# The last step of an output product by accumulator, and the residual scaled half by half inside the product

## The chip, the cores and the metric

The kernel runs on one core of a Trainium2 chip. The metric is the device time of one execution in microseconds (us); the median of three runs stands for it. One execution was also recorded by the hardware profiler; all rows below are of it.

## The reference, cut to what matters

A diffusion transformer of two layers works on 512 tokens (x) and 256 context tokens, each 1024 wide. Every layer has a feed-forward network (FFN), a set of four mixers, and a second FFN. What concerns the change is how a sublayer's result is joined to the stream, and the FFN itself:

```python
ALPHA = (2 * DEPTH) ** 0.25

def post_norm(x, f, g, b):
    return layer_norm(ALPHA * x + f, g, b)

def swiglu(h, w_in, w_out):
    a, u = jnp.split(h @ w_in, 2, axis=-1)
    return (jax.nn.silu(a) * u) @ w_out
```

So after each sublayer the stream x is scaled by ALPHA, the sublayer's output f (multiplied by a row of the modulation) is added, and the sum is normalised with a gain g and a bias b. D_FF is 2816, which is 22 chunks of 128.

## The kernel before, in words

The stream lies in SBUF as six tiles of 128 tokens by 1024, `res`: t0 to t3 hold x, t4 and t5 the context. The last FFN works on x alone, with four tiles.

All products are in fp32 by three matmuls each: every operand is split into a high part and the rest, and `mm3` (L335 to L337) issues high times high, high times low, low times high. For weights the split is made on the fly: SP loads `wraw` (two buffers), ScalarE (ACT) casts `wh` (L328), VectorE (DVE) subtracts to give `wl` (L329); there are six slots of each. GpSimd (POOL) adds and subtracts weight tiles in the FFN's input product, which uses a fast scheme with sums of tiles (`first`, `winograd`, L573, L608 to L616); its results are combined on DVE (L692 to L703).

`ffn` runs the 22 chunks in parts: 0 to 4, 4 to 8, 8 to 12, 12 to 16, 16 to 18 and 18 to 22 (the last FFN: 0 to 6, 6 to 12, 12 to 18, 18 to 22). For each chunk it makes the gated product and stores it as `gTh` (ACT, L646) and `gTl` (DVE, L647). After each part but the last it calls `branch_out`, the output product of this part: for each half of 512 columns (dh 0, then 1), steps of two chunks; in each step for both chunks, for all tiles, three matmuls. Six accumulators are open in a half: t0 and t1 in single-bank PSUM tiles (`psp`, two buffers), t2 and t4 in one two-bank tile and t3 and t5 in another (`ps`, two buffers). When a half's matmuls are issued, `add` follows for each tile: DVE multiplies the accumulator by the modulation row (L472) and adds the result to `res` (L474). There are 15 such calls in the four FFNs. The merges behind the mixers call the same function.

The residual of a sublayer is the normalised stream, scaled. Normalisation without gain and bias goes to the next product; `res` is brought to ALPHA times (x g + b) by `rescale`: two gain rows are loaded (L451), scaled on ACT (L460), and then for both halves and all tiles DVE multiplies and adds (L465), 24 instructions with six tiles, 16 with four. For the kernel's first sublayer `scale_input` only multiplies by ALPHA (L359, six instructions of 1024 columns). Either one is a generator kept as `self.behind`, and `ffn` runs it to its end ahead of its first output product:

```python
            if lo == 0:
                for _ in self.behind(pool, tiles):
                    pass
```

The order of each engine is not written by hand: a scheduler walks the program and puts an instruction where its operands and buffers are thought to be ready, so what stands late in the code can run early. That is how the scaling got to the start of the FFN, between the casts of the next stream (L391, L392), the small rows of the normalisation (L398 to L436) and the combinations of the input product. Each engine then runs its own order strictly, and waits at an instruction whose operands or buffers are not ready.

In the third mixer (`gqa`) small tables of cosines times gain are made on POOL (L862, L866), twelve instructions in all.

## Time and profile before

| | us |
|---|---|
| median of three runs | 2946.29 |
| lowest and highest | 2943.25, 2949.76 |
| the profiled execution | 2945.09 |
| its span in the profile | 2943.3 |
| PE busy | 2844.5 (97%) |
| DVE busy | 2062.5 (70%) |
| ACT busy | 1196.5 (41%) |
| POOL busy | 460.5 (16%) |
| mean granted clock of TensorE | 0.991 of full speed |

PE (TensorE) is busy nearly always, so the table says little; the places where it waits, and for whom, are read from the list of waits and the timelines in the section on the rows. Two hints for them: a matmul of 512 columns is shown with 0.39 us or so, but matmuls overlap and start 0.23 us apart; and an idle time in brackets names the engine, tile and line that ended it.

### The profile page before, as it was taken

What the parts mean: (1) busy time and instruction counts of PE and PEld (TensorE: products, weight loads), DVE (VectorE), ACT (ScalarE), POOL (GpSimd) and SP (SyncE); (2) the same over time, 40 slices, a digit from 0 to 9 for tenths busy, and PEclk for the clock granted to TensorE, in tenths of its full rate; (3) what the DMA queues carried; (4) which work ended last, traced back from release to release, by engine and by line L of the source; (5) the groups of instructions that cost most, each with busy time, mean ns of one, the idle gap of its engine ahead of it and who ended that gap; (6) DMA issues with size and microseconds to landing.
All of it is one profiled execution on the core that took longest, in us unless ns stands there. A gap on an engine that the chain in (4) does not pass through costs nothing.

```text
span 2943.3 us, 43403 instructions
## 1 busy us (share of the span) xinstructions
PE 2844.5 (97%) x16220; PEld 2437.0 (83%) x16220; DVE 2062.5 (70%) x4278; ACT 1196.5 (41%) x2269; POOL 460.5 (16%) x342
## 2 busy tenths in 40 slices
PE   7999999999999999999999999999999999899997
PEld 4898888988787788888888789998988787788886
DVE  4766658775757787666676976776886767876558
ACT  4333233364456552322323523332344456443333
POOL 1222122100000012221121222221200000012112
PEclk9999999999999999999999999999999999999998
DMA  6453334231133313543444122222132242242332
GB/s 233 144 165 108 108 107 130 85 110 51 47 77 72 108 58 108 186 136 116 158 135 138 58 72 72 79 61 76 48 98 72 57 110 78 79 129 88 94 99 71
DMA packets 319207, 296.07 MB, mean 101 GB/s; under 512 B 16312, under 2 KB 244752, under 8 KB 318740
## 3 DMA queue, kind: packets, MB, share of 16 engines
q1 hardware_dynamic: 317939, 290.80, 31.9%
q0 software_dynamic: 1056, 2.49, 0.4%
q8 instruction: 128, 2.10, 0.3%
q14 instruction: 84, 0.68, 0.1%
HBM read 270.52 MB, written 7.39 MB: 94 GB/s over the span
## 4 chain that ended last, share of the span: by engine, by line
PE 78%; DVE 14%; issue 3%; ACT 2%; DMA 2%; POOL 0%; SPq 0%; DVEq 0%; ACTq 0%; POOLq 0%
PE ps L335 12%; PE ps L337 12%; PE ps L336 12%; PE psp L335 9%; PE psp L337 9%; PE psp L336 9%; PE ps L260 2%; PE ps L1033 2%; PE ps L1075 2%; PE psp L1091 2%; DVE wl L329 2%; DVE tmp L472 2%; DVE res L465 2%; DVE res L474 1%; DVE actl L392 1%
## 5 line engine op out<-in xcount | busy, mean ns | idle before, releaser
L328 ACT CAST wh<-wraw 128x512 fp32r<-128x512 f32 x570 | 352.3, 621 | 874.0 <-PE ps L337 454.9
L329 DVE TENSOR_TENSOR wl<-wraw,wh 128x512 fp32r<-128x512 f32 x570 | 414.8, 733 | 323.7 <-ACT wh L328 316.3
L335 PE MATMUL psp<-acth,wh 128*128 128x384 f32 (+2 forms) x1432 | 482.1, 337 | 8.3 <-DVE e L701 3.8
L336 PE MATMUL psp<-actl,wh 128*128 128x384 f32 (+2 forms) x1432 | 480.3, 336 | 4.8 <-DVE actl L392 4.7
L337 PE MATMUL psp<-acth,wl 128*128 128x384 f32 (+2 forms) x1432 | 478.6, 335 | 5.2 <-DVE wl L329 5.2
L335 PEld LDWEIGHTS psp<-acth,wh 128*128 128x128 f32 x1432 | 271.3, 190 | 48.9 <-issue 25.4
L328 ACT CAST wh<-wrax 128x512 fp32r<-128x512 f32 x280 | 173.8, 622 | 338.1 <-PE ps L336 198.0
L336 PEld LDWEIGHTS psp<-actl,wh 128*128 128x128 f32 x1432 | 271.7, 190 | 19.9 <-DVE actl L392 6.5
L337 PEld LDWEIGHTS psp<-acth,wl 128*128 128x128 f32 x1432 | 271.8, 190 | 17.7 <-DVE wl L329 5.8
L335 PE MATMUL ps<-S,wh 128*128 128x384 f32 (+1 forms) x840 | 275.9, 329 | 8.1 <-DVE e L692 5.3
L337 PE MATMUL ps<-S,wl 128*128 128x384 f32 (+1 forms) x840 | 275.1, 327 | 0.0
L336 PE MATMUL ps<-S,wh 128*128 128x384 f32 (+1 forms) x840 | 275.0, 327 | 0.0
L329 DVE TENSOR_TENSOR wl<-wrax,wh 128x512 fp32r<-128x512 f32 x280 | 214.1, 770 | 84.5 <-ACT wh L328 59.3
L335 PE MATMUL ps<-acth,wh 128*128 128x512 f32 (+2 forms) x688 | 245.8, 359 | 3.2 <-ACT wh L328 1.7
L336 PE MATMUL ps<-actl,wh 128*128 128x512 f32 (+2 forms) x688 | 244.3, 355 | 0.0
L337 PE MATMUL ps<-acth,wl 128*128 128x512 f32 (+2 forms) x688 | 243.5, 354 | 0.0
L335 PE MATMUL ps<-wh,gTh 128*128 128x512 f32 x594 | 234.9, 395 | 7.5 <-DVE tmp L472 7.5
L337 PE MATMUL ps<-wh,gTl 128*128 128x512 f32 x594 | 233.5, 393 | 0.0
L336 PE MATMUL ps<-wl,gTh 128*128 128x512 f32 x594 | 233.3, 393 | 0.0
L474 DVE TENSOR_TENSOR res<-res,tmp 128x512 f32<-128x512 f32 x268 | 188.0, 732 | 0.6
L335 PEld LDWEIGHTS ps<-S,wh 128*128 128x128 f32 x840 | 158.7, 189 | 12.9 <-issue 6.9
L336 PEld LDWEIGHTS ps<-S,wh 128*128 128x128 f32 x840 | 158.7, 189 | 0.0
(385 smaller groups left out, 5452.2 us busy)
## 6 DMA issues: line engine op xcount, KB each, us to landing
araw<-in_ada_w_dram SPq DMA_DIRECT2D x128, 512.0 KB
wraw<-in_ffn_w_out_dram SPq DMA_DIRECT2D x88, 512.0 KB
wrax<-in_ffn_w_in_dram SPq DMA_DIRECT2D x160, 256.0 KB
wraw<-in_ffn_w_in_dram SPq DMA_DIRECT2D x120, 256.0 KB
wraw<-in_mix_w_in_dram SPq DMA_DIRECT2D x44, 512.0 KB
wraw<-in_ffn_w_in_dram SPq DMA_DIRECT2D x36, 512.0 KB
wraw<-in_mix_w_out_dram SPq DMA_DIRECT2D x16, 512.0 KB
mrow<-mrow SPq DMA_DIRECT2D x10, 512.0 KB
```

The lines of the kernel that those rows point to most:

```text
L260: nc.tensor.matmul(ps[32 * g:32 * g + 32, :], lhsT=self.cs[:, k, c0:c0 + 32], rhs=w[:, k - kk, :], start=i == 0 and k < 4, stop=i == len(n ...
L328: self.nc.scalar.copy(h, raw)
L329: self.nc.vector.tensor_tensor(lo, raw, h.bitcast(F32), op=ALU.subtract)
L335: mm(out, lhsT=a[0], rhs=b[0], start=start, stop=False)
L336: mm(out, lhsT=a[0], rhs=b[1], start=False, stop=False)
L337: return mm(out, lhsT=a[1], rhs=b[0], start=False, stop=stop)
L465: nc.vector.tensor_tensor(r, r, x[:, lo:hi], op=op)
L472: nc.vector.tensor_tensor(y, acc, mrow[0 if t < 4 else 1][:, dh * 512:(dh + 1) * 512], op=ALU.mult)
L474: nc.vector.tensor_tensor(r, r, y, op=ALU.add)
L1033: nc.tensor.matmul(ps[:, at:at + hi - lo], lhsT=q, rhs=part[:, lo:hi], start=i == 0, stop=i == 1)
L1075: nc.tensor.transpose(pt[:, j * P:(j + 1) * P], p[:, a:a + P], self.ident)
L1091: nc.tensor.matmul(out[64 * a:64 * a + 64, :], lhsT=v[:, kt, vcol:vcol + 64], rhs=pT[:, i], start=i == 0, stop=i == len(order) - 1)
```

## The change

It has three parts. First, in the last step of a half in `branch_out` the matmuls are sorted by tile and then by chunk: each accumulator gets both chunks of the step one after the other. Second, `rescale` and `scale_input` are cut into a first piece (gain loads and ACT's scaling) and one piece for each half; `ffn` runs the first piece ahead of the first output product, and `branch_out` runs a half's piece behind the matmuls of that half and ahead of its additions, and not before the subtraction of the part's last `gTl` has been issued. `scale_input` now has twelve instructions of 512 columns. Third, the tables of the third mixer are made on DVE.

```diff
-    def scale_input(self, pool, tiles):
-        for r in self.res:
-            self.nc.vector.tensor_scalar(r, r, ALPHA, None, op0=ALU.mult)
+    def scale_input(self, pool, tiles, tags=None):
+        yield
+        for lo, hi in ((0, 512), (512, D)):
+            for t in tiles:
+                r = self.res[t][:, lo:hi]
+                self.nc.vector.tensor_scalar(r, r, ALPHA, None, op0=ALU.mult)
             yield
...
         for x in gb:
             nc.scalar.mul(x, x, ALPHA)
+        yield
         for lo, hi in ((0, 512), (512, D)):
...
-    def branch_out(self, l, i, tiles, steps, a_of, w_of, mrow, tmp, todo=None):
+    def branch_out(self, l, i, tiles, steps, a_of, w_of, mrow, tmp, todo=None, behind=None):
...
-                for j, k in enumerate(s):
-                    for t in tiles:
-                        self.mm3(acc[t], a_of(k, t), w[j], k == chunks[0], k == chunks[-1])
+                by_step = [(t, j) for j in range(len(s)) for t in tiles]
+
+                for t, j in sorted(by_step) if s is steps[-1] else by_step:
+                    self.mm3(acc[t], a_of(s[j], t), w[j], s[j] == chunks[0], s[j] == chunks[-1])
+            if behind:
+                with self.tc.issue_after(behind[1].ins):
+                    next(behind[0])
...
-                store(g, f, lo)
+                end = store(g, f, lo)
+            behind = None
             if lo == 0:
-                for _ in self.behind(pool, tiles):
-                    pass
+                behind = self.behind(pool, tiles, ("mrow0", "mrow1") if self.side else ("mrow1", "mrow2")), end
+                next(behind[0])
...
-            nc.gpsimd.tensor_tensor(tc_, cos, bcast1(gain, 4), op=ALU.mult)
+            nc.vector.tensor_tensor(tc_, cos, bcast1(gain, 4), op=ALU.mult)
...
-                nc.gpsimd.tensor_tensor(t5[:, :, :, f], s5[:, :, :, f], bcast1(g5[:, :, 1 - f], 8), op=ALU.mult)
+                nc.vector.tensor_tensor(t5[:, :, :, f], s5[:, :, :, f], bcast1(g5[:, :, 1 - f], 8), op=ALU.mult)
```

Three places show how the orders move. In the changed kernel the same code has other line numbers: L465 becomes L469, L472 L476, L474 L478, L392 L395, L402 L405. The first place is on PE, the beginning of the last step of the first half in the first output product of the kernel. The names end in running numbers; two `wh` numbers are the two chunks of the step, `psp` and `ps` the accumulators. Before:

```order
474 L335 MATMUL psp_1029<-wh_1081,gTh_395 128x512
475 L336 MATMUL psp_1029<-wl_1082,gTh_395 128x512
476 L337 MATMUL psp_1029<-wh_1081,gTl_396 128x512
477 L335 MATMUL psp_1030<-wh_1081,gTh_395 128x512
478 L336 MATMUL psp_1030<-wl_1082,gTh_395 128x512
479 L337 MATMUL psp_1030<-wh_1081,gTl_396 128x512
480 L335 MATMUL ps_197_1031<-wh_1081,gTh_395 128x512
481 L336 MATMUL ps_197_1031<-wl_1082,gTh_395 128x512
482 L337 MATMUL ps_197_1031<-wh_1081,gTl_396 128x512
```

Each accumulator gets three matmuls of the first chunk and then the next one's turn comes. The same place on PE after the change:

```order
474 L335 MATMUL psp_1023<-wh_1075,gTh_395 128x512
475 L336 MATMUL psp_1023<-wl_1076,gTh_395 128x512
476 L337 MATMUL psp_1023<-wh_1075,gTl_396 128x512
477 L335 MATMUL psp_1023<-wh_1079,gTh_395 128x512
478 L336 MATMUL psp_1023<-wl_1080,gTh_395 128x512
479 L337 MATMUL psp_1023<-wh_1079,gTl_396 128x512
480 L335 MATMUL psp_1024<-wh_1075,gTh_395 128x512
481 L336 MATMUL psp_1024<-wl_1076,gTh_395 128x512
482 L337 MATMUL psp_1024<-wh_1075,gTl_396 128x512
```

The matmuls of the second chunk (1079) moved up behind those of the first, so the first accumulator has all its matmuls after six. The second place is on DVE, near the start of the second FFN, before; `rs` are the small rows of the normalisation, `mrow` the scaled gain and bias:

```order
1613 L465 TENSOR_TENSOR res_2001_9931<-res_2001_9931,mrow_2220_11217 128x512
1614 L403 SCALAR_TENSOR_TENSOR rs_2110_10540<-rs_2110_10540,rs_2108_10538 128x2
1615 L465 TENSOR_TENSOR res_2002_9932<-res_2002_9932,mrow_2220_11217 128x512
1616 L404 SCALAR_TENSOR_TENSOR rs_2109_10539<-rs_2110_10540,rs_2109_10539 128x2
1617 L465 TENSOR_TENSOR res_2001_9931<-res_2001_9931,mrow_2221_11218 128x512
1618 L402 TENSOR_TENSOR rs_2110_10540<-rs_2109_10539 128x2
```

Scaling stands between the rows of the normalisation. The same place on DVE after the change:

```order
1622 L329 TENSOR_TENSOR wl_10692<-wraw_10685,wh_10691 128x512
1623 L405 TENSOR_TENSOR rs_2110_10546<-rs_2109_10545 128x2
1624 L406 SCALAR_TENSOR_TENSOR rs_2110_10546<-rs_2110_10546,rs_2108_10544 128x2
1625 L407 SCALAR_TENSOR_TENSOR rs_2109_10545<-rs_2110_10546,rs_2109_10545 128x2
1626 L405 TENSOR_TENSOR rs_2110_10546<-rs_2109_10545 128x2
```

All 24 scaling instructions of this FFN moved from its start. The third place is where they went: DVE in the first output product of the second FFN. Before, from the part's last `gTl` to the additions of the first half:

```order
1732 L647 TENSOR_TENSOR gTl_10606<-ffg_11072,gTh_10605 128x768
1733 L329 TENSOR_TENSOR wl_11418<-wraw_11415,wh_11417 128x512
1734 L329 TENSOR_TENSOR wl_11422<-wraw_11415,wh_11421 128x512
1735 L329 TENSOR_TENSOR wl_11493<-wraw_11486,wh_11492 128x512
1736 L472 TENSOR_TENSOR tmp_11347<-psp_11251,mrow_2222_11247 128x512
1737 L472 TENSOR_TENSOR tmp_11350<-psp_11252,mrow_2222_11247 128x512
1738 L474 TENSOR_TENSOR res_2001_9931<-res_2001_9931,tmp_11347 128x512
1739 L474 TENSOR_TENSOR res_2002_9932<-res_2002_9932,tmp_11350 128x512
1740 L472 TENSOR_TENSOR tmp_11353<-ps_2226_11253,mrow_2222_11247 128x512
```

After the change, where the last `gTl` is row 1719 and the half's twelve scaling instructions are rows 1720 to 1731:

```order
1730 L469 TENSOR_TENSOR res_2005_9941<-res_2005_9941,mrow_2221_11224 128x512
1731 L469 TENSOR_TENSOR res_2006_9942<-res_2006_9942,mrow_2221_11224 128x512
1732 L476 TENSOR_TENSOR tmp_11341<-psp_11233,mrow_2222_11229 128x512
1733 L476 TENSOR_TENSOR tmp_11344<-psp_11234,mrow_2222_11229 128x512
1734 L478 TENSOR_TENSOR res_2001_9937<-res_2001_9937,tmp_11341 128x512
1735 L478 TENSOR_TENSOR res_2002_9938<-res_2002_9938,tmp_11344 128x512
1736 L329 TENSOR_TENSOR wl_11412<-wraw_11409,wh_11411 128x512
1737 L329 TENSOR_TENSOR wl_11416<-wraw_11409,wh_11415 128x512
1738 L469 TENSOR_TENSOR res_2001_9937<-res_2001_9937,mrow_2220_11223 128x512
1739 L476 TENSOR_TENSOR tmp_11347<-ps_2226_11235,mrow_2222_11229 128x512
```

The scaling moved in between `gTl` and the first multiply, and the two weight subtractions of the second half (`wl_11412` and `wl_11416`, before `wl_11418` and `wl_11422`) moved behind the first two additions.

## Rows read from the trace of the kernel before

**Rows 1.** The page: busy time, share, instructions; and the chain that ended last.

```profile
PE 2844.5 (97%) x16220; PEld 2437.0 (83%) x16220; DVE 2062.5 (70%) x4278; ACT 1196.5 (41%) x2269; POOL 460.5 (16%) x342
...
PE 78%; DVE 14%; issue 3%; ACT 2%; DMA 2%; POOL 0%; SPq 0%; DVEq 0%; ACTq 0%; POOLq 0%
```

**Rows 2.** PE's waits by releaser: us in total, times, longest.

```profile
PE ps L335 <- DVE tmp L472: 8.6, 16, 0.8
PE ps L335 <- DVE e L692: 5.3, 4, 1.9
PE psp L335 <- DVE e L701: 5.2, 5, 1.9
PE psp L337 <- DVE wl L329: 5.2, 2, 3.0
PE psp L336 <- DVE actl L392: 4.7, 6, 1.6
...
PE ps L335 <- DVE ffg L642: 2.8, 1, 2.8
```

**Rows 3.** Timeline of DVE, first product of FFN 1: start, us, instruction, count.

```profile
128.65 1.28 DVE L472 TENSOR_TENSOR tmp<-psp,mrow 128x512 f32<-128x512 f32 x2
...
133.35 1.28 DVE L474 TENSOR_TENSOR res<-res,tmp 128x512 f32<-128x512 f32 x2
134.55 1.27 DVE L472 TENSOR_TENSOR tmp<-ps,mrow 128x512 f32<-128x512 f32 x2
```

**Rows 4.** Timeline of PE at the second half, FFN 1 and FFN 2.

```profile
134.17 0.39 PE L336 MATMUL psp<-wl,gTh 128*128 128x512 f32 x1
135.28 0.50 PE L335 MATMUL ps<-wh,gTh 128*128 128x512 f32 x1 [0.72 <-DVE tmp L472]
135.62 0.39 PE L336 MATMUL ps<-wl,gTh 128*128 128x512 f32 x1
...
1158.15 0.39 PE L335 MATMUL psp<-wh,gTh 128*128 128x512 f32 x1
...
1162.10 0.50 PE L335 MATMUL ps<-wh,gTh 128*128 128x512 f32 x1 [0.53 <-DVE tmp L472]
```

**Rows 5.** Timeline of DVE at the start of FFN 2: two groups of scaling.

```profile
1078.76 3.08 DVE L465 TENSOR_TENSOR res<-res,mrow 128x512 f32<-128x512 f32 x5
...
1116.88 0.68 DVE L465 TENSOR_TENSOR res<-res,mrow 128x512 f32<-128x512 f32 x1
```

**Rows 6.** Timeline of PE at the start of FFN 2: two of its waits.

```profile
1088.37 0.39 PE L336 MATMUL psp<-actl,wh 128*128 128x256 f32 x1 [1.11 <-DVE actl L392]
...
1106.82 0.44 PE L337 MATMUL psp<-acth,wl 128*128 128x384 f32 x1 [2.18 <-DVE wl L329]
```

**Rows 7.** By stretch: us, busy PE, PEld, DVE, ACT, POOL, granted clock, DMA, GB/s.

```profile
1082.00:1104.00 22.00, 19.84 (x134) 17.71 (x134) 22.00 (x42) 15.23 (x34) 7.27 (x5) 1.00 0.09 25
1104.00:1118.00 14.00, 10.10 (x48) 9.46 (x46) 12.17 (x18) 6.04 (x11) 7.94 (x5) 0.88 0.39 114
...
1682.00:1694.00 12.00, 9.47 (x44) 9.15 (x44) 10.18 (x13) 5.46 (x10) 7.26 (x5) 0.86 0.34 101
...
2600.00:2631.00 31.00, 28.42 (x181) 26.23 (x182) 22.66 (x40) 12.78 (x24) 7.42 (x5) 0.94 0.49 155
```

**Rows 8.** Timeline of PE in the one-step product of FFN 3.

```profile
2066.62 0.79 PE L337 MATMUL psp<-wh,gTl 128*128 128x512 f32 x1 [1.22 <-DVE gTl L647]
2067.21 0.63 PE L335 MATMUL psp<-wh,gTh 128*128 128x512 f32 x1
```

**Rows 9.** Timeline of DVE in the first product of FFN 2.

```profile
1144.48 0.96 DVE L647 TENSOR_TENSOR gTl<-ffg,gTh 128x768 fp32r<-128x768 f32 x1 [0.30 <-ACT gTh L646]
...
1156.66 2.38 DVE L474 TENSOR_TENSOR res<-res,tmp 128x512 f32<-128x512 f32 x2
```

**Rows 10.** Timeline of POOL in the first product of FFN 2.

```profile
1155.21 1.49 POOL L608 TENSOR_TENSOR wraw<-wraw,wraw 128x512 f32<-128x512 f32 x1 [18.49 <-DMA wraw<-in_ffn_w_in_dram]
```

**Rows 11.** POOL's groups: one of the four of tables; busy, mean ns.

```profile
L866 POOL TENSOR_TENSOR tab<-cst,kn 128x256 f32<-128x256 f32 x4 | 4.2, 1066 | 0.9 <-DVE tA L802 0.9
```

More of the change, by code (lines that the diff above doesn't have):

```diff
@@ L646, in store @@
             nc.scalar.copy(gh, g)
-            nc.vector.tensor_tensor(gl, g, gh.bitcast(F32), op=ALU.subtract)
+            return nc.vector.tensor_tensor(gl, g, gh.bitcast(F32), op=ALU.subtract)
         def first(late):
@@ L736, in ffn @@
                                                .rearrange("(j p) c -> p j c", p=P), (2, 512)),
-                    mrow, pool)
+                    mrow, pool, behind=behind)
                 continue
```

## Prediction

> **What bounds the kernel now.** I read the page first. TensorE (PE) is busy for 97% of the span and PE alone makes up 78% of the chain that ended last; VectorE (DVE) makes up 14% of it [rows 1]. So this is a kernel that runs matmuls nearly all the time, and any gain must come out of the short stretches in which PE waits. I went next to the list of PE's waits and took from it the six that the change can touch [rows 2]; all six end on DVE. They fall into two kinds.
>
> The first kind is the 8.6 us in 16 waits for the multiply of L472 (accumulator times modulation row). They stand where an output product goes from its first half of 512 columns to its second. In the first product of the first feed-forward network (FFN) DVE's rows read as a queue: t0 and t1 multiplied, added, then t2 and t3, and only from 134.55 the multiplies of t4 and t5 [rows 3]. Tiles t2 and t4 share one two-bank PSUM tile, so the second half's t2 cannot start before t4's multiply is done: PE starts a matmul at 134.17 and the next at 135.28 [rows 4]. Between two starts there are 0.23 us on an undisturbed stretch, so this wait costs 1.11 - 0.23 = 0.88 us, and 0.11 more in the matmul after it (0.34 between starts), 0.99 in all against the 0.72 that the row shows as idle. I add 0.28 us per wait for this wherever I use idle times. In the second FFN the same place is 0.53 idle [rows 4].
>
> The second kind is DVE's backlog at the start of an FFN. There the scaling of the residual stands between work that PE needs: in the second FFN five scaling instructions in a row end at 1081.8 in front of the casts, and others alternate with the sums of the FFN's input product [rows 5]. The table by stretch has DVE busy for all 22.00 us from 1082 to 1104 [rows 7], and PE waits for it at 1088.37 and 1106.82, 1.11 and 2.18 us, among others [rows 6].
>
> **Part 1, the last step by accumulator.** It adds and removes no instruction; 36 matmuls of the last step stand in another order. Before, t0 is complete after 21 of them and t5 after 36, three matmuls (0.69 us) apart; now t0 is complete after 6 and each next one 1.4 us later. DVE takes about 1.2 us for one accumulator (a pair of multiplies takes 1.28, a pair of additions the same when nothing disturbs it [rows 3]), so it keeps pace and the queue is gone: t4 is complete 1.4 us before the end of the half, its multiply ends some 0.5 us before or up to 0.6 after that end, depending on the additions in between, and PE wants that tile after seven more matmuls, 1.6 us after the end. t5's has 2 us. The waits of this kind should vanish. 16 x 0.28 + 8.6 = 13.1 us are there; one of the 16 (0.8 us) belongs to the second merge, whose DVE queue holds a scaling that stays, which leaves 12.3. In the first product of each of the four FFNs the scaling now stands in the queue, and I count half of their waits (four of about 0.8, so 1.6 us) as kept: **10.7 us gained**. Bounds 7 (nothing in first products, and a fifth of the rest kept) and 12.3.
>
> **Part 2, the scaling leaves the starts.** The scaling itself hardly changes: 24 instructions per FFN with six tiles, 16 with four, 0.60 us from start to start (five took 3.08 [rows 5]); in the first FFN six of 1024 columns become twelve of 512. What counts is the place. From the starts of the second and third FFN 14.4 us of DVE work goes, from the fourth 9.6. The waits that end on this backlog are four for e of L692 (5.3 us), five for e of L701 (5.2; two of them, 1.9 each, at FFN starts, so I take 3.8), two for wl (5.2), six for actl (4.7) and one for ffg (2.8) [rows 2]: 21.8 us in 15 waits, with 0.28 each 26.0. To that comes TensorE's clock. In the stretch from 1104 to 1118, after idling 2.18 us, PE was granted 0.88 of full speed on average; the stretches at 1682 and 2600 show 0.86 and 0.94 [rows 7]. A mean of 0.88 of 2.4 GHz is 24% of 14 us at the 1.2 GHz level, which loses half of 3.4 us, 1.7; the other two lose 1.7 and 1.9. Together 31.3 us. Not all of it will be had, because a removed wait uncovers the next one: ACT's casts (a weight's wl waits for wh on its row all through the kernel), POOL's sums of weights, and the FFN's own latency from product to gate to product. DVE loses 38.4 us of work in the three stretches to save 31, and it was busy without a gap there, so most should come through; I take 85%: **27 us gained**, bounds 13 (the next wait ends half as late) and 31.
>
> **What part 2 costs where it goes.** In the first product of the second FFN the last gTl ends at 1145.4 [rows 9], 4 us after the product's first matmul (1141.5; the second half starts at 1158.2, which is 72 matmuls of 0.23 later). Then DVE runs the 12 instructions of the half, 7.2 us, until 1152.6. t0 and t1 are complete at 1151.2 and 1152.6, so the multiplies start without delay; two multiplies and two additions bring DVE to 1155.0, and the two weight subtractions that now stand behind them to 1156.2, ahead of 1158.2, when PE's second half reads the first of them. t2, t3 and t4 follow with two scaling instructions of the second half mixed in, and t4's multiply ends at about 1159.9; PE wants its tile at 1159.8. So the cover is used up but hardly overdrawn. I charge 0.5 us per FFN, **2 us** in all. It is a knife's edge: each us by which DVE is late there costs one, and up to 10 us are possible if POOL gets in the way (below). Queued behind the scaling on DVE are also the release of the weight buffers for SP (weights of the next chunk, about 5 us later than now) and of the gain rows: in the second FFN SP now waits for these with four loads of the modulation product, which go out after the second half's scaling. Their data is read in the next chunk, after the product, so I charge nothing; if they land late, it is a few us.
>
> **The short parts.** Chunks 16 and 17 form a product of one step. With the new order PE no longer runs all six tiles of chunk 16 first, but reaches the first matmul that needs chunk 17's gTl as the 15th instead of the 21st. PE already waits for gTl there, in the third FFN 1.22 us at 2066.62, and the matmuls after it take 0.63 us instead of 0.40 [rows 8]. There are three such products. Reaching gTl up to six matmuls sooner (1.4 us, less a matmul of another line that now stands between) makes each wait about 0.7 longer: **2.1 us lost**; between 0 (if the sooner start of chunk 16's matmuls hides it) and 3.3.
>
> **Part 3, the tables.** Twelve multiplies of 256 columns go from POOL, where one took 1.07 us [rows 11], to DVE, where I put one at 0.4 (0.6 for 512 columns, with a fixed part). That is 5 us of DVE in two mixer phases, beside POOL chains that are off the path. I charge **0.7 us**, between a gain of 1 and a loss of 2.
>
> **Sum.** 10.7 + 27 - 2 - 2.1 - 0.7 = 32.9 us. Against the profiled execution's 2945.1 us that gives 2912.2; the median of the runs shown is 2946.3, 1.2 us above it, so **2913 us**. All favourable ends at once: 2946.3 - (12.3 + 31 + 1) = 2902. All unfavourable ones: gains 7 + 13, costs 10 + 3.3 + 2, 2942.
>
> **Rivals.** (a) The scaling meets POOL. In the first product POOL sums weights, 1.49 us at 1155.21 and a second sum behind it [rows 10], and the pair of additions that ran at that time took 2.38 us instead of 1.28 [rows 9]. The 24 scaling instructions read two operands from SBUF as these additions do. If both sums hold DVE up by 1.1 to 2 us in each half, the knife's edge gives way and PE waits 2 us in each half of the first products of three FFNs, 12 us: 2925. For it: the rows; against it: the load that starts these sums is itself issued later. The Trainium skill, page "SBUF — State Buffer", section "Who interferes with whom", says that a DVE instruction with two SBUF inputs contends with a GpSimd instruction that reads SBUF, and that the later of the two fully blocks. By that rule the rival's delay would be a whole POOL instruction each time, some 3 us per half where two meet it, 2931 instead of 2925; the pair of 2.38 shows a delay but less than a whole instruction.
>
> (b) The starts stay bound. With DVE's backlog gone, ACT's casts or POOL's sums end the same waits half as late: part 2 gives 13 instead of 27, so 2927. For it: PE's rows at these places name a release that itself waited for ACT. Against it: DVE was busy without a gap.
>
> (c) Only the accumulators work: the waits at the starts belong to the FFN's own latency, the scaling was merely filling. 2946.3 - 10.7 + 4.8 = 2940.4, at the edge of no change. Against it: a DVE that is merely filling would show idle time, and it has none from 1082 to 1104 [rows 7].
>
> (d) Slower: the scaling lies bare in the product. If gTl of the last chunk ended only when t1 is complete (7 us later than in rows 9), or DVE entered the product that late, all 7.2 us of a half would stand between PE's accumulators and their release, 14.4 + 14.4 + 9.6 + 7.2 = 45.6 us over four FFNs, against 37.7 gained and 2.8 of the other costs: 2957. It decides from a delay of about 6 us on; nothing in the rows delays DVE by that much.
>
> **How the numbers follow.** My forecast, 2905 to 2921, gets 0.55; (a) 0.2; (b) 0.15; (c) 0.05; (d) 0.03; better than 2905 0.02. The range reaches from the favourable end over (a) and most of (b): 2902 to 2935. Faster means by over 0.2% (5.9 us, about what a measurement of this kernel can tell from no change): all but (c) and (d), 0.92; same 0.05; slower 0.03.
>
> **What the new profile would show.** Part 1: waits of PE on the multiply of L472 (new line L476) fall from 16 to a few, all in first products or the merge. Part 2: no scaling rows before the first product, DVE no longer at 22.00 of 22 behind the start, waits on e, actl and ffg below 6 us, the granted clock at 1.00 there. Costs: the three waits on gTl in the one-step parts at 1.7 to 2 us; t4's multiply in first products within 1 us of PE's wish. The forecast is wrong if waits on wl, the casts of ACT or POOL's sums replace those at the starts, or if first products show waits of over 2 us.

## The result, and the profile after

The changed kernel takes 2913.84 us (median of 4 runs, 2912.34 to 2915.91), the kernel before on the same chip 2945.26. The ratio is 0.9892, with a 95% interval from 0.9875 to 0.9909: 31 us less. 2913 was forecast. The profiled execution took 2912.34 us. That the sum came out does not say that its terms did; the rest of this text takes it apart.

The page of the changed kernel, first part, answers to [rows 1]:

```profile
PE 2834.7 (97%) x16220; PEld 2432.6 (84%) x16220; DVE 2089.9 (72%) x4296; ACT 1195.6 (41%) x2269; POOL 440.5 (15%) x330
```

PE has the same 16220 matmuls. DVE even has 27 us more work than before, and yet the gain comes from it: what matters is where its work stands. The list of PE's waits (us in total, times, longest) answers to [rows 2]; L335 waits for L476 (before L472), L701 (L692), L710 (L701), L651 (L642) and L395 (L392):

```profile
PE ps L335 <- DVE e L701: 4.0, 2, 2.4
...
PE ps L335 <- DVE ffg L651: 2.1, 2, 1.1
PE psp L335 <- DVE e L710: 2.0, 4, 0.7
...
PE ps L335 <- DVE tmp L476: 1.3, 3, 0.6
PE psp L336 <- DVE actl L395: 1.3, 4, 0.6
...
PE psp L335 <- DVE tmp L476: 1.2, 2, 0.6
```

The waits for the accumulators' multiply fell from 8.6 us in 16 to 1.3 in 3 (the two with `psp` belong to the second layer's merge and are as before). Of the five kinds at the FFN starts the two for wl are gone, the others fell from 18.0 us (5.3, 5.2, 4.7, 2.8) to 9.4. The same stretches of the two traces don't hold the same work any more, but three stretches behind the starts of the second, third and fourth FFN show the kind of change (columns as in [rows 7]):

```profile
1082.00:1104.00 22.00, 21.06 (x134) 19.65 (x134) 17.78 (x32) 11.96 (x24) 8.09 (x4) 1.00 0.23 64
1660.00:1682.00 22.00, 18.51 (x92) 17.37 (x91) 19.55 (x30) 10.03 (x20) 8.93 (x7) 0.92 0.31 96
2572.00:2600.00 28.00, 28.00 (x192) 26.10 (x191) 18.57 (x33) 12.30 (x23) 7.41 (x5) 1.00 0.40 119
```

DVE is no longer busy without a gap (17.78 of 22, before 22.00), and in the fourth FFN PE runs through. But the stretch in the third FFN still has 3.5 us of idle PE and a granted clock of 0.92.

Since PE runs the same number of matmuls in both kernels, the start of the n-th one in either trace tells how much has been saved by that point. Matmuls are counted from 0. Within a product the order differs and a single point can be off by 1 us; the points below lie between products, but for no. 6552.

| matmul no. | place | before, us | after, us | saved | step |
|---|---|---|---|---|---|
| 396 | behind the start of FFN 1 | 92.1 | 90.2 | 1.9 | 1.9 |
| 2196 | behind its fourth product | 431.5 | 426.7 | 4.8 | 2.9 |
| 2520 | behind its one-step product | 495.1 | 490.5 | 4.7 | -0.1 |
| 4320 | in the first layer's mixers | 810.7 | 804.6 | 6.1 | 1.5 |
| 6408 | behind the start of FFN 2 | 1134.1 | 1121.5 | 12.6 | 6.5 |
| 6552 | in its first product | 1165.9 | 1152.5 | 13.4 | 0.8 |
| 6732 | in the chunks behind it | 1200.0 | 1188.3 | 11.7 | -1.7 |
| 8208 | behind its fourth product | 1473.0 | 1459.0 | 14.0 | 2.3 |
| 8964 | behind its one-step product | 1612.8 | 1598.4 | 14.4 | 0.4 |
| 9432 | behind the start of FFN 3 | 1710.5 | 1690.0 | 20.5 | 6.1 |
| 9684 | behind its first product | 1763.5 | 1744.1 | 19.4 | -1.1 |
| 11016 | behind its fourth product | 2020.0 | 1998.2 | 21.8 | 2.5 |
| 11268 | behind its one-step product | 2072.9 | 2048.8 | 24.1 | 2.3 |
| 12636 | in the second layer's mixers | 2326.5 | 2300.6 | 25.9 | 1.8 |
| 14472 | behind the start of FFN 4 | 2606.1 | 2575.0 | 31.1 | 5.2 |
| 16219 | the last | 2922.3 | 2889.5 | 32.8 | 1.7 |

### The profile page after: what moved, and what is told of

Its sections match the earlier page's. It is cut to its first block, busy times and chain, and to the rows that moved or that the text cites. A ratio compares the mean times of both kernels' runs of the same rounds, so it can differ in the third digit from the quotient of the medians.

```text
span 2910.6 us, 43301 instructions
## 1 busy us (share of the span) xinstructions
PE 2834.7 (97%) x16220; PEld 2432.6 (84%) x16220; DVE 2089.9 (72%) x4296; ACT 1195.6 (41%) x2269; POOL 440.5 (15%) x330
## 5 line engine op out<-in xcount | busy, mean ns | idle before, releaser
L329 DVE TENSOR_TENSOR wl<-wraw,wh 128x512 fp32r<-128x512 f32 x570 | 428.4, 757 | 194.9 <-ACT wh L328 185.7
L335 PE MATMUL psp<-acth,wh 128*128 128x384 f32 (+2 forms) x1432 | 481.1, 336 | 4.7 <-DVE dqT L916 2.4
L335 PEld LDWEIGHTS psp<-acth,wh 128*128 128x128 f32 x1432 | 270.4, 189 | 44.7 <-issue 26.3
L329 DVE TENSOR_TENSOR wl<-wrax,wh 128x512 fp32r<-128x512 f32 x280 | 226.2, 810 | 83.0 <-ACT wh L328 42.1
L335 PE MATMUL ps<-S,wh 128*128 128x384 f32 (+1 forms) x840 | 276.0, 329 | 7.1 <-DVE e L701 4.0
L337 PEld LDWEIGHTS psp<-acth,wl 128*128 128x128 f32 x1432 | 270.5, 189 | 11.7 <-issue 1.9
L335 PE MATMUL ps<-acth,wh 128*128 128x512 f32 (+2 forms) x688 | 246.0, 359 | 1.7 <-ACT wh L328 1.7
L335 PE MATMUL ps<-wh,gTh 128*128 128x512 f32 x594 | 233.3, 393 | 0.9 <-DVE tmp L476 0.9
L478 DVE TENSOR_TENSOR res<-res,tmp 128x512 f32<-128x512 f32 x268 | 187.1, 711 | 3.3
L335 PEld LDWEIGHTS ps<-S,wh 128*128 128x128 f32 x840 | 158.6, 189 | 12.1 <-DVE e L701 4.6
L476 DVE TENSOR_TENSOR tmp<-ps,mrow 128x512 f32<-128x512 f32 x174 | 116.7, 686 | 61.0 <-PE ps L337 60.5
```

Source lines behind the costliest of these rows:

```text
L329: self.nc.vector.tensor_tensor(lo, raw, h.bitcast(F32), op=ALU.subtract)
L335: mm(out, lhsT=a[0], rhs=b[0], start=start, stop=False)
L337: return mm(out, lhsT=a[1], rhs=b[0], start=False, stop=stop)
L476: nc.vector.tensor_tensor(y, acc, mrow[0 if t < 4 else 1][:, dh * 512:(dh + 1) * 512], op=ALU.mult)
L478: nc.vector.tensor_tensor(r, r, y, op=ALU.add)
```

## Each part alone

The theory on record is that the early accumulators and the move of the scaling each act where they stand, at the second halves and at the FFN starts, and that their gains add. Its rivals: the starts owe their gain to the accumulators, or the move alone does nothing for the starts. Three kernels carry one part each.

Part 1 alone, on the kernel before:

```diff
-                for j, k in enumerate(s):
-                    for t in tiles:
-                        self.mm3(acc[t], a_of(k, t), w[j], k == chunks[0], k == chunks[-1])
+                by_step = [(t, j) for j in range(len(s)) for t in tiles]
+                for t, j in sorted(by_step) if s is steps[-1] else by_step:
+                    self.mm3(acc[t], a_of(s[j], t), w[j], s[j] == chunks[0], s[j] == chunks[-1])
```

> Part 1 alone, on the kernel before: the last step of each half by accumulator, scaling and tables as they were. If the parts add up as in the prediction, the 15 waits for L472 at the second halves go (12.3 us) and the one-step products lose 2.1: about 2935, against 2945 of before. The comparison of the traces gives the one-step products no loss and would have 2934. If the starts of the FFNs owe their gain to the earlier accumulators and not to the scaling's move (rival c turned round), this kernel has most of the whole gain: 2920 or less.

Measured: 2932.96 us against 2944.48, ratio 0.9958 (0.9943 to 0.9973), 11.5 us less. PE's waits in its trace:

```profile
PE ps L335 <- DVE e L692: 6.3, 4, 2.7
PE psp L336 <- DVE actl L392: 5.6, 6, 1.9
PE psp L337 <- DVE wl L329: 4.4, 2, 2.3
```

The waits at the starts are as in [rows 2], and the one for L472 has left the head of the list. The accumulators do nothing for the starts.

Part 2 alone, the changed kernel with the accumulators filled in turn and the tables on POOL:

```diff
-                for t, j in sorted(by_step) if s is steps[-1] else by_step:
+                for t, j in by_step:
...
-            nc.vector.tensor_tensor(tc_, cos, bcast1(gain, 4), op=ALU.mult)
+            nc.gpsimd.tensor_tensor(tc_, cos, bcast1(gain, 4), op=ALU.mult)
...
```

> Part 2 alone: scaling half by half in the first products, accumulators filled in turn as before, tables on POOL. If the gain at the FFN starts is that of the scaling's move: 20 us less than before, about 2925, with the waits for L472 at 13 to 16 as before. If the scaling needs the early accumulators as cover (t0 complete only 3.5 us before the end of the half), nothing changes for it, since DVE is through with it before that; but the prediction's working says that t4's multiply comes at least 1 us later in first products, so at most 4 us are lost again: 2929. By rival c 2943.

Measured: 2920.65 us against 2944.48, ratio 0.9919 (0.9904 to 0.9934), 23.8 us less. Its list of waits keeps the first kind and has the second reduced just as in the changed kernel:

```profile
PE ps L335 <- DVE tmp L476: 7.9, 15, 1.0
...
PE ps L335 <- DVE e L701: 4.0, 2, 2.4
```

By position it saves 6.7 us up to behind the start of the second FFN, where the changed kernel saves 6.5, 4.4 in the start of the third up to the point where the changed kernel saves 4.4, and 5.0 in the fourth (matmuls 14436 to 14472), as there. So the gain at the starts is that of the move, and rival (c) is out.

Part 3 alone:

```diff
-            nc.gpsimd.tensor_tensor(tc_, cos, bcast1(gain, 4), op=ALU.mult)
+            nc.vector.tensor_tensor(tc_, cos, bcast1(gain, 4), op=ALU.mult)
...
-                nc.gpsimd.tensor_tensor(t5[:, :, :, f], s5[:, :, :, f], bcast1(g5[:, :, 1 - f], 8), op=ALU.mult)
+                nc.vector.tensor_tensor(t5[:, :, :, f], s5[:, :, :, f], bcast1(g5[:, :, 1 - f], 8), op=ALU.mult)
```

> Part 3 alone: the twelve table multiplies on DVE. The prediction charged 0.7 us: 2946. The trace after shows the waits of PE in the third mixer shorter (1.16 to 0.59 in the second layer): 1 to 1.5 us gained, 2944. Both lie within what the comparison can tell; the profile's position at the end of the mixers tells them apart.

Measured: 2943.94 us against 2944.48, ratio 0.9997 (0.9987 to 1.0006): no change that the medians can tell. The positions tell more. In the second layer's mixers this trace gains 1.2 us between matmuls 11880 and 11916 and 0.6 between 12600 and 12636, and so does every other trace with the tables on DVE, the changed kernel's too (1.8 us in all). Parts 1 and 2 alone, with the tables on POOL, gain 0.0 and 0.4 at the first place and nothing at the second. In the kernel before, POOL, DVE and PE read at the first place:

```profile
2190.62 1.80 POOL L866 TENSOR_TENSOR tab<-cst,qn 128x256 f32<-128x256 f32 x2
```

```profile
2190.26 1.57 DVE L392 TENSOR_TENSOR actl<-S,acth 128x256 fp32r<-128x256 f32 x2 [0.47 <-ACT acth L391]
2191.76 0.81 DVE L391 CAST acth<-S 128x256 fp32r<-128x256 f32 x1
```

```profile
2192.62 0.39 PE L335 MATMUL ps<-acth,wh 128*128 128x256 f32 x1 [0.77 <-DVE acth L391]
```

With the tables gone from there, DVE's pair takes 0.76 and the cast 0.3, and PE's wait is not in the trace. At the second place PE's wait for a tile of the third mixer fell from 1.16 to 0.59. So part 3 is a small gain, not a loss.

The three alone make 11.5 + 23.8 + 0.5 = 35.8 us, together they give 31 to 32; the intervals, some 4 us to either side for each part, do not separate the two. The positions show one overlap: both parts alone win the same 0.8 us at the second half of the first product, in the second and in the third FFN, and together they win it once (0.8 and 0.3). Behind these products the changed kernel's trace loses 1.7 and 1.4 us and part 2's 0.1 and 0.7, but the second trace of the changed kernel (last of the experiments) loses only 0.2 at the first of the two places, so that difference is not shown to be the parts'.

## The one-step products

The changed kernel with the products of chunks 16 and 17 in the old order:

```diff
-                for t, j in sorted(by_step) if s is steps[-1] else by_step:
+                for t, j in sorted(by_step) if s is steps[-1] and len(steps) > 1 else by_step:
```

> The changed kernel, but products of a single step (chunks 16 and 17, three of them) fill their accumulators in turn as before. By the prediction's 2.1 us of loss this wins 2 us: 2912. If the loss does not exist, as the positions in the trace after suggest, it is the same or up to 2 us slower: 2914 to 2916.

Measured: 2912.59 us against 2944.48, ratio 0.9893 (0.9877 to 0.991), the same as the changed kernel's 0.9892. These intervals are too wide for a loss of 2.1 us; the positions (end of this section) say that it is not there. The trace of the changed kernel shows why, in the first FFN's one-step product:

```profile
474.62 1.04 PE L260 MATMUL ps<-araw,cs 128*32 128x512 f32 x2
...
475.93 0.50 PE L335 MATMUL psp<-wh,gTh 128*128 128x512 f32 x1 [0.26 <-ACT gTh L655]
...
477.61 0.50 PE L337 MATMUL psp<-wh,gTl 128*128 128x512 f32 x1 [0.95 <-DVE gTl L656]
```

The matmuls of L260 (of the modulation) stand ahead of the wait now, where they cost nothing. Before, they broke into the product later, and a pair took about 1 us of PE's time:

```profile
489.02 1.04 PE L260 MATMUL ps<-araw,cs 128*32 128x512 f32 x2
489.99 0.50 PE L335 MATMUL ps<-wh,gTh 128*128 128x512 f32 x1
```

So the wait is about as long as before, 0.26 + 0.95 against 1.11 idle, and what was moved into it pays for the rest. By position the first two such products lose 0.1 to 0.2 us each.

## What the scaling costs in its new place

The changed kernel without the scaling in the products, and with it doubled:

```diff
-            if behind:
-                with self.tc.issue_after(behind[1].ins):
-                    next(behind[0])
```

> The changed kernel without the 76 scaling instructions of the four FFNs on DVE (the residual is not scaled there; the gain rows are still loaded and scaled by ACT). What it gains over the changed kernel is what the scaling costs in its new place. By the prediction (0.5 us per FFN and half of four boundary waits, 2 + 1.6 us) 2910; by rival a, POOL's sums in the way, 12 us: 2902. If waits behind the first products (modulation loads, ACT) come from the scaling too, between the two.

Measured: 2908.88 us against 2944.12, ratio 0.9886 (0.987 to 0.9903). In the two traces' positions it is 3.4 us ahead of the changed kernel at the end; the ratios differ by 0.0006, 1.8 us, well inside both intervals. The gains by position stand behind the first products, 2.8 us in the second FFN (1.2 against the second trace of the changed kernel) and 1.3 in the third, and in the first products, 0.8 in the first FFN and 0.5 in the third. Differences at places without scaling, up to 2.1 us either way, stand beside them, so the 3.4 is good to about 2.

```diff
...
                     nc.vector.tensor_tensor(r, r, x[:, lo:hi], op=op)
+                    if tags2 is None:
+                        nc.vector.tensor_tensor(r, r, r, op=ALU.max)
...
```

(`tags2` is set by the merges alone, whose scaling is not doubled.)

> The changed kernel with the scaling of the second, third and fourth FFN's first products doubled: each of its instructions is followed by one of the same size with two operands in SBUF that changes nothing (maximum of a tile with itself); 64 more instructions of 0.6 us, 38 us of DVE. By the prediction's working DVE has no slack left in these products (the knife's edge: each us later costs one) and all of the first halves' share, 7.2 + 7.2 + 4.8 us, plus a good part of the second halves' comes back: 2938 to 2952. If PE had more slack there than was worked out, less than 10 us: under 2924.

Measured: 2942.93 us against 2944.12, ratio 0.9998 (0.9989 to 1.0007): 29 us of the gain are gone, for 38 us more of DVE work. This is the delay of rival (d), brought about by more work. By position 4.1 and 3.5 us are lost up to the second half of the second and the third FFN's first product, 6.6 and 11.6 behind that, and 4.3 in the fourth FFN. So there is little slack, but the price of a delay is not the same everywhere.

In the changed kernel DVE's rows in the second FFN's first product run as the prediction had them (start, us, instruction, count):

```profile
1131.85 0.96 DVE L656 TENSOR_TENSOR gTl<-ffg,gTh 128x768 fp32r<-128x768 f32 x1 [0.30 <-ACT gTh L655]
1132.72 7.30 DVE L469 TENSOR_TENSOR res<-res,mrow 128x512 f32<-128x512 f32 x12
1139.95 1.28 DVE L476 TENSOR_TENSOR tmp<-psp,mrow 128x512 f32<-128x512 f32 x2
...
1146.13 1.28 DVE L476 TENSOR_TENSOR tmp<-ps,mrow 128x512 f32<-128x512 f32 x2
```

and PE's, at the end of the first half and where it wants t2's tile back:

```profile
1145.52 0.39 PE L335 MATMUL psp<-wh,gTh 128*128 128x512 f32 x1
...
1148.08 0.40 PE L335 MATMUL ps<-wh,gTh 128*128 128x512 f32 x1
```

Twelve scaling instructions took 7.30 us, and t4's multiply (the second of the pair at 1146.13) ended at about 1147.4, 1.9 us after the end of the half; 1.7 was forecast. PE wanted the tile 2.6 us after it, not 1.6, because eleven matmuls on t0 and t1 ran ahead of it and not the seven that were counted, so there was no wait at all. With the scaling doubled the same place reads (the multiply's line is L478 in that kernel):

```profile
1148.13 0.50 PE L335 MATMUL psp<-wh,gTh 128*128 128x512 f32 x1 [2.22 <-DVE tmp L478]
...
1149.64 0.63 PE L335 MATMUL psp<-wh,gTh 128*128 128x512 f32 x1
```

PE waits for t0's multiply already, and after that idle stretch its matmuls take 0.63 us with 0.43 between starts, instead of 0.39 and 0.23: the 1.2 GHz level. From 1146 to 1154 the granted clock averages 0.79:

```profile
1146.00:1154.00 8.00, 5.87 (x18) 4.47 (x19) 8.00 (x15) 0.00 (x0) 0.00 (x0) 0.79 0.01 2
```

In the third FFN the cover was not enough, because POOL's first sum met DVE's additions, as rival (a) has it (DVE, POOL and PE of the changed kernel):

```profile
1716.21 2.38 DVE L478 TENSOR_TENSOR res<-res,tmp 128x512 f32<-128x512 f32 x2
```

```profile
1716.48 1.55 POOL L617 TENSOR_TENSOR wraw<-wraw,wraw 128x512 f32<-128x512 f32 x1 [24.62 <-DVE tmp L476]
```

```profile
1719.25 0.51 PE L335 MATMUL ps<-wh,gTh 128*128 128x512 f32 x1 [0.27 <-DVE tmp L476]
```

In the first FFN a POOL sum from 128.59 on stretched an addition at 128.88 to 1.57 us, and PE waited 0.64 at 131.69. In the kernel with the doubled scaling, which has the same scaling as the changed kernel in this FFN, the sum there began behind the addition, the addition took 0.69, and there was no such wait.

More of the cost lies behind the product. In the second FFN a set of modulation weights comes just too late for PE; in the third PE waits for ACT's gate:

```profile
1180.62 1.05 PE L260 MATMUL ps<-araw,cs 128*32 128x512 f32 x4 [0.27 <-DMA araw<-in_ada_w_dram]
...
1741.29 0.41 PE L335 MATMUL ps<-S,wh 128*128 128x384 f32 x1 [1.10 <-ACT ffg L699]
```

There are four such rows of L260, each with 0.24 to 0.33 of idle time and slower restarts; without the scaling the sixteen matmuls run without a break. The second trace of the changed kernel has two such waits instead of four. By SP's timeline these loads go out right behind the next chunk's weights, whose buffers DVE frees behind the scaling: 2.2 us behind them in the changed kernel (1169.60 and 1171.79), 5.6 us without the scaling (1166.83 and 1172.41), so that there the two sets of loads overlap less. That the overlap delays them was not tried by itself.

## What took the scaling's place at the starts

The starts gave less than forecast. In the changed kernel's trace the third FFN still has a wait of 2.36 us; the rows of DVE, POOL and PE around it (three queries of the timeline, one fence each):

```profile
1673.27 1.41 DVE L329 TENSOR_TENSOR wl<-wrax,wh 128x512 fp32r<-128x512 f32 x1
1674.60 0.54 DVE L701 TENSOR_TENSOR e<-ps,e 128x384 f32<-128x384 f32 x1
```

```profile
1672.86 1.27 POOL L617 TENSOR_TENSOR wrax<-wrax,wrax 128x512 f32<-128x512 f32 x1 [5.72 <-DMA wrax<-in_ffn_w_in_dram]
```

```profile
1675.20 0.44 PE L335 MATMUL ps<-S,wh 128*128 128x384 f32 x1 [2.36 <-DVE e L701]
```

A weight subtraction beside a POOL sum took 1.41 us instead of 0.69, and PE waited for the combination behind it. Is POOL what now bounds the start? The changed kernel without POOL's sums for chunks 2 and 3:

```diff
-        tt = nc.gpsimd.tensor_tensor
+        tt = nc.gpsimd.tensor_tensor if f > 3 else lambda *a, **k: None
```

> The changed kernel without POOL's sums of weight tiles for chunks 2 and 3 (28 instructions; these chunks get the tiles as loaded, so the result of the chunks is another; no other instruction moves). The changed kernel still waits some 4 us at the start of the second and of the third FFN, where DVE's weight subtractions run 1.3 to 1.6 us instead of 0.7. If POOL's sums are what took the place of the scaling there (they hold DVE up, or deliver late), 5 to 8 us go: 2906 to 2909. If the waits are the FFN's own latency or ACT's casts: unchanged, 2913.

Measured: 2904.02 us against 2944.12, ratio 0.9866 (0.9851 to 0.9881). By position it gains 4.1 us on the changed kernel at the start of the second FFN and 5.6 at the third's; the waits for ffg and for e of L701 are gone. POOL's sums are what remained. The same place in this kernel's timeline of DVE:

```profile
1667.93 0.68 DVE L329 TENSOR_TENSOR wl<-wrax,wh 128x512 fp32r<-128x512 f32 x1
1668.53 0.55 DVE L701 TENSOR_TENSOR e<-ps,e 128x384 f32<-128x384 f32 x1
```

Do the sums hold DVE up, or do they deliver late? The next kernel lets POOL make them, but nobody uses them:

```diff
-        put("T2", x[:, 0])
+        put("T2", y[:, 0] if f < 4 else x[:, 0])
         put("B22", y[:, 1])
-        put("T3", x[:, 1])
+        put("T3", y[:, 1] if f < 4 else x[:, 1])
+        if f < 4:
+            put("T4", y[:, 0])
+            put("T1", y[:, 1])
         tt(y[:, 0], y[:, 0], x[:, 0], op=ALU.subtract)
-        put("T4", y[:, 0])
+        if f > 3:
+            put("T4", y[:, 0])
         tt(y[:, 1], y[:, 1], x[:, 0], op=ALU.subtract)
-        put("T1", y[:, 1])
+        if f > 3:
+            put("T1", y[:, 1])
```

> As the run without POOL's sums of chunks 2 and 3 (2904), but POOL still does them, into the same tiles at about the same time; only the weights that ACT and DVE split for these chunks are taken from tiles as loaded (so these chunks' result is another), and nobody waits for POOL. If the sums hold the start up because DVE's two-operand instructions are slowed while POOL works, the gain of that run is lost again: 2911 to 2914. If they hold it up because they deliver late, the gain stays: 2904 to 2906.

Measured: 2910.62 us against 2944.53, ratio 0.9886 (0.9872 to 0.9901), close to the changed kernel on the same chip (below, 2912.08). Read by what was expected, the loss would be DVE being held up. But the positions speak otherwise: 3.9 of 4.1 us of gain at the second start and 4.0 of 5.6 at the third remain. Of the 5.6 us by which this trace ends behind that without the sums, 2.1 are lost in the third FFN's one-step product, where single executions differ anyway (last section), and 1.4 and 1.5 are lost behind the two starts, where POOL's idle sums, now later than in the changed kernel, stretch DVE's subtractions. Its timelines of DVE and of POOL there:

```profile
1670.76 1.19 DVE L329 TENSOR_TENSOR wl<-wrax,wh 128x512 fp32r<-128x512 f32 x1
...
1672.34 1.31 DVE L329 TENSOR_TENSOR wl<-wrax,wh 128x512 fp32r<-128x512 f32 x1
```

```profile
1671.36 1.75 POOL L629 TENSOR_TENSOR wraw<-wraw,wraw 128x512 f32<-128x512 f32 x1
1673.07 1.74 POOL L618 TENSOR_TENSOR wrax<-wrax 128x512 f32<-128x512 f32 x1
```

Both effects exist, then: the subtractions take 1.2 to 1.3 us beside a POOL sum whose result nobody wants, and at the start itself the gain mostly stays when nobody waits for the sums. In which parts, this run does not settle, since the sums moved.

Either way the remedy is to take the first of these sums off POOL:

```diff
-        tt = nc.gpsimd.tensor_tensor
+        tt = (nc.vector if f == 2 else nc.gpsimd).tensor_tensor
```

> The changed kernel with the sums of chunk 2 made on DVE instead of POOL (12 instructions in three FFNs): a sum then takes about 0.6 us instead of 1.3 to 1.9, and no POOL instruction runs beside DVE's at that place; DVE gets 2.4 us more work in each of these starts. If POOL's sums are what bounds the starts now: 2906 to 2910. If DVE's own work bounds them: 2914 to 2918.

Measured: 2906.36 us against 2944.53, ratio 0.9873 (0.9857 to 0.989). With chunk 3 as well:

```diff
-        tt = nc.gpsimd.tensor_tensor
+        tt = (nc.vector if f in (2, 3) else nc.gpsimd).tensor_tensor
```

> As the run before, with the sums of chunk 3 on DVE too (28 instructions in four FFNs). Chunk 3 comes after the backlog, where DVE has idle time and POOL's sums are ahead of their use: no change against the run with chunk 2 alone if only the start is bound, within 2 us; 3 to 5 us less if POOL's sums of chunk 3 hold up the combinations of chunk 2 on DVE.

Measured: 2908.86 us, ratio 0.9879 (0.9864 to 0.9894). The changed kernel itself on this chip:

> The changed kernel itself, on the chip of these runs, for comparison: 2914.

Measured: 2912.08 us against 2944.53, ratio 0.9892 (0.9877 to 0.9907). The sums of chunk 2 on DVE bring 5.7 us more than the change, with intervals that still overlap, but each of its four runs (2905.39 to 2909.28) lies below each of the changed kernel's four on this chip (2909.50 to 2915.86); by position the gain is 3.8 us at the second start and 3.6 at the third. Chunk 3 adds nothing. With chunk 2 alone this is the lowest median of the kernels here that leave no work out.

## A move that did not pay

The second layer's merge still has its scaling ahead of the product. The same treatment for it:

```diff
...
-        for _ in self.behind(tmp, tiles, ("mrow1", "mrow2") if last else ("mrow0", "mrow1")):
-            pass
+        behind = self.behind(tmp, tiles, ("mrow1", "mrow2") if last else ("mrow0", "mrow1"))
+        next(behind)
...
-            mrow, tmp, self.turns(self.mod_affine(l, 1), tmp, tiles))
+            mrow, tmp, self.turns(self.mod_affine(l, 1), tmp, tiles), behind=(behind, None))
```

> The changed kernel with the same move for the second layer's merge, whose scaling the change left ahead of the product: a half's scaling behind the half's matmuls. Its eight scaling instructions of the second half go behind the first half's additions on DVE. The three waits for L476 in this merge (0.6, 0.5 and 0.4 us idle, some 2 us with what follows) should go: 2912. If the first merge product's additions were late for another reason (eight scaling instructions still stand ahead of them): unchanged, 2914.

Measured: 2916.13 us against 2944.12, ratio 0.9908 (0.9893 to 0.9923), nothing gained. The three waits for L476 did go and by position some 2.4 us with them, but right behind that, still in the merge, this kernel falls 6.8 us behind, and its timeline of PE names new waits:

```profile
2507.31 0.50 PE L336 MATMUL psp<-wl,acth 128*128 128x512 f32 x1 [2.34 <-DVE wl L329]
...
2515.41 0.50 PE L335 MATMUL psp<-wh,acth 128*128 128x512 f32 x1 [2.49 <-ACT wh L328]
```

The eight instructions now stand on DVE ahead of a weight subtraction that PE wants at once. A scaling that is moved needs a place where nothing urgent queues behind it, and the merge has none.

## Why the prediction was right, point by point

The sum, 2913, holds; the views from which it was made name the right places, and no rival took over, though (a) and (b) each came true in part. Term by term:

- **Early accumulators, 10.7 us forecast.** By position the products gain 2.9, 3.1, 2.5 and 1.7 us in the four FFNs, 10.2. Right in mechanism and size. Alone the part brings 11.5.
- **The starts, 27 us forecast.** By position 1.9 + 6.5 + 6.1 + 5.2 = 19.7, and 19.4 in the second trace (0.5 of the 1.9 is won before matmul 360, and the traces of parts 1 and 3 alone have it too). The mechanism is right (part 2 alone); mis-sized is the step that took 85% of 31.3 us, because "most should come through". It was 63%. The argument failed that DVE, busy without a gap, was the only limit: part of its busy time was itself stretched by POOL, and what stood next was POOL's sums of chunk 2, which the prediction named under (b) but gave a small chance. Without them 4.1 and 5.6 us more come through. Its own signs showed it: the waits on e, actl and ffg are 9.4 us and not below 6, and the clock at the third start is 0.92.
- **The scaling in the products, 2 us and half of four boundary waits (1.6).** Measured 3.4 us by position, with about 2 us of doubt. In the second FFN t4's multiply came within 0.2 us of its forecast, but PE wanted it 1 us later than worked out, and no wait came of it; there the objection to rival (a) held, POOL's first sum started at 1148.12, after the half. In the first and the third FFN the sum met the additions, and PE waited 0.64 and 0.27 us: rival (a)'s mechanism, far below its 12 us. More is paid behind the products, at the modulation loads for which nothing was charged, and at ACT's gate.
- **The knife's edge.** Doubling the scaling costs 29 us for 38, 0.75 per us of delay on average and not 1, and most of it is lost behind the first halves, not at the place that was worked out.
- **One-step products, 2.1 us of loss.** Measured 0.1 to 0.2 in two of three (the third below). The step looked at how many matmuls stand ahead of gTl, and did not see that the scheduler put matmuls of another line into the wait.
- **Tables, 0.7 us of loss.** The medians cannot tell, but by position the sign was wrong: they gain 1.8 us in the second layer, more than the bound of 1. The step charged DVE's extra work and put nothing down for DVE no longer meeting POOL there.

Against the forecast the starts are 7.3 us short, and the products and what lies behind them 1.4. The one-step products give 4.6 more than forecast and the mixers 4.0, and so the sum comes out. Of these 8.6 us 3.8 are not the change's: 2.3 at the third FFN's one-step product (next section but one) and 1.5 in the first layer's mixers. There PE waits 2.4 us for the same instruction in the trace of before and in both of the changed kernel; behind it the kernel before and the second trace of the changed kernel run their next matmuls 0.43 us apart, at the 1.2 GHz level, and the first trace of the changed kernel does not. The second trace has neither gain and saves 29.2 us at its end, not 32.8. A part of the agreement is luck.

## What to carry to other kernels

Work that nobody waits for still costs what it delays: look where an engine that is "not the bottleneck" runs without a gap, and move its fillers to a place where their successors have slack, then count that slack, since here doubling the moved work cost 29 of the 31 us gained. Order the last matmuls so that results come out one by one, at the pace of the engine that drains them. And when a backlog is removed, price what stands second there (here the partner engine's sums) before taking most of the wait as gained. A single trace can be off by several us in places that the change does not touch, so take a second one of the same kernel before giving each place its term.

## What was not expected of the hardware

A subtraction with two operands in SBUF took 1.2 to 1.4 us instead of 0.69 in the rows above when a POOL sum ran beside it, also when nobody used POOL's result. The Trainium skill, page "SBUF — State Buffer", section "Who interferes with whom", says that a DVE instruction with two SBUF inputs contends with a GpSimd instruction that reads SBUF, and calls the ports that the two share an exclusive lock. The rows agree: 1.41 us at 1673.27, where the POOL sum ends at 1674.13 and the subtraction is through 0.55 us later, so most of its own 0.69 came behind the sum.

Where the two meet, single executions differ by 2 to 3 us, and with them TensorE's clock. In the kernel with the tables alone, whose order at these places is that of the kernel before, the half-speed matmuls of [rows 8] stand in the second FFN's one-step product and not in the third's. Its timelines of DVE and of POOL there:

```profile
1516.24 1.69 DVE L702 TENSOR_TENSOR ffg<-ffg,e 128x384 f32<-128x384 f32 x1
1517.85 1.64 DVE L703 TENSOR_TENSOR ffg<-ffg,e 128x384 f32<-128x384 f32 x1
...
1520.40 1.93 DVE L647 TENSOR_TENSOR gTl<-ffg,gTh 128x768 fp32r<-128x768 f32 x1 [0.30 <-ACT gTh L646]
```

```profile
1516.22 1.30 POOL L608 TENSOR_TENSOR wraw<-wraw,wraw 128x512 f32<-128x512 f32 x1 [4.74 <-DMA wraw<-in_ffn_w_in_dram]
```

In the kernel before at the same place:

```profile
1517.21 0.55 DVE L702 TENSOR_TENSOR ffg<-ffg,e 128x384 f32<-128x384 f32 x1
1517.68 1.64 DVE L703 TENSOR_TENSOR ffg<-ffg,e 128x384 f32<-128x384 f32 x1
...
1520.95 0.94 DVE L647 TENSOR_TENSOR gTl<-ffg,gTh 128x768 fp32r<-128x768 f32 x1
```

```profile
1517.39 1.52 POOL L608 TENSOR_TENSOR wraw<-wraw,wraw 128x512 f32<-128x512 f32 x1 [4.52 <-DVE e L701]
```

In the first case POOL, whose row names the load as its releaser, began 0.02 us ahead of DVE's first addition, and both additions and gTl, links of one chain to PE, were stretched; in the second POOL began 0.18 us behind it, and only one was. In the first case PE then waits twice, about 1 and 1.2 us, and goes on at the 1.2 GHz level, as in [rows 8]. The changed kernel has the same choice in the third FFN: in the trace shown here its stretch from 2040 to 2072 has a granted clock of 1.00, in the second trace of it (last of the experiments) 0.95 with a wait of 2.31 us, and that one loses 2.8 us there against the first (first fence the one, second fence the other):

```profile
2040.00:2072.00 32.00, 30.52 (x154) 27.10 (x153) 29.51 (x44) 9.00 (x15) 11.35 (x8) 1.00 0.11 33
```

```profile
2040.00:2072.00 32.00, 29.14 (x137) 25.29 (x136) 27.83 (x41) 7.23 (x12) 9.51 (x7) 0.95 0.12 33
```

So the 2.3 us that the changed kernel's trace gains at this place are not the change's, and a difference of that size between two single traces is no evidence where POOL and DVE meet.
